# Two layers of a hybrid encoder trunk: the FFN's down-projection groups of 4, 4, 5, 5, 4 chunks in place of 5, 5, 5, 4, 3

## The chip, the core and the metric

One NeuronCore of a Trainium2 chip runs the whole kernel. The metric is the device time of one execution in microseconds (us). The kernel before takes 1569.97 us, the median of three runs between 1569.14 and 1570.35.

## What is computed

The reference runs two layers over 512 tokens of width 1024, in float32. A layer is a normalised input, three branches (two kinds of attention and a pooling branch), gates, an output projection, and then the part that the change touches, a gated MLP with 2816 hidden channels:

```python
hf = rms_norm(x, ffn_norm_g[l])
u = depthwise_conv(hf @ ffn_w_up[l], ffn_conv_w[l], ffn_conv_b[l])
u_gate, u_val = u[..., :D_FF], u[..., D_FF:]
x = x + (jax.nn.silu(u_gate) * u_val) @ ffn_w_down[l]
```

## The kernel before

**Layout.** Activations stand with channels on the 128 partitions and the 512 tokens along the row. A float32 product is made of three reduced-precision ones: each operand is split into a high part (`wh`, `HH`, `ah`) and the rest (`wl`, `HL`, `al`), and `mm3` (lines 530 to 533) issues high by high, high by low and low by high. So every weight tile that arrives by DMA (`raw`, line 403) is split before TensorE can use it. ScalarE (ACT) makes the high half. The low half comes in one of three ways: a subtraction on GpSimd or VectorE (line 458), the same subtraction on VectorE for weights that VectorE has just summed (line 492), or `by_transfer` (lines 428 to 435), where ACT writes the negated high half and GpSimd's queue issues an accumulating DMA that adds the raw weight on top (line 434).

**The FFN.** The 2816 hidden channels are 22 chunks of 128. Each chunk has a gate part and a value part, both 1024 deep. They are made in one of two ways:

- A *plain* chunk (`plain`, line 1686): two parts one after the other, each 8 weight tiles by `mm3` on 512 columns, so 24 matmuls of 512 columns for a part. Each part goes into one PSUM bank, in turn of the tags acc, ST, AV with two banks each. VectorE scales it by the normalisation factor `rbc` (line 1695), and `convolve` (line 1664) follows.
- A *pair* (`product`, line 1701): gate and value of a chunk by Winograd's seven products of a 2 by 2 block multiplication, in the order 11, 12, 1, 22, 2, 4, 3. Each product is 4 weight tiles by `mm3` on 256 columns: 12 matmuls of 256 columns. Three of the seven weight blocks are split by transfer (`fh`, `fl`, slots of their own), four are sums or differences that VectorE makes first (line 486). ACT sets partial products aside (`sx`, line 1728), VectorE adds them up (line 1736).

`convolve` is a chain that goes back and forth between ACT and VectorE: ACT scales (`a<-u`), VectorE adds the two neighbours (line 307, two instructions), ACT applies silu to a gate part; for a value part VectorE multiplies by the gate (`a<-a,a`), ACT writes the high half of the result (`act` or `ah`), VectorE the low half (`act` or `al`). Then TensorE may use the chunk.

**Groups.** The down projection needs all 22 chunks for each of its 8 output tiles, so it is done in groups: group g's chunks go into a PSUM bank (tags mi and S, in turn), 8 output tiles of as many blocks as the group has chunks; a block is three matmuls of 512 columns. VectorE then adds the bank to `XM` (line 1806). `SIZES` gives the chunks of each group. Group 0's chunks are plain, all others are pairs. The blocks of group g are dealt over the pairs of group g + 1, behind the products 22, 2, 4 and 3 of each pair; the order is written out by `_ffn` (lines 112 to 131):

```python
SIZES = (5, 5, 5, 4, 3)
PLACE = (0, 5, 0, 5, 0)
...
dealt = len(late) - (KEEP * SIZES[g - 1] if g == len(SIZES) - 1 else 0)
...
now = late[:dealt * (n + 1) // (c1 - c0) - dealt * n // (c1 - c0)]
...
late += [("d", g, m, i) for m in range(KC) for i in range(c1 - c0)]
```

Of the next to last group two output tiles' worth of blocks (`KEEP` is 2) is kept until after the last pair; then the last group's blocks follow. `PLACE` says where a group's finished chunks lie: `PLACE[g] + i` of 6 places, and past those in tiles of two other pools.

**Order and queues.** Each engine works through its own list in order. The lists are written by the program itself with a modelled clock (`Clock`, line 205), which decides the order in which chains of steps are emitted. Weights are split ahead of their use: 4 units ahead while plain units are near, 6 once a pair's unit comes within reach (line 515). SyncE (SP) issues the weights' DMAs in order; the first pairs' raw weights are fetched early, one 256 KB block after a plain part (line 155).

Of the kernel before, what the change touches and what calls it, by code (L numbers as in the profile page):

```python
# [40 lines left out]
PRE_A = 16  # L41
PRE_B = 8
LA, LAP, LAF = 3, 4, 6
SIZES = (5, 5, 5, 4, 3)
PLACE = (0, 5, 0, 5, 0)
ROOM = 6
KEEP = 2
FORMS = ("11", "12", "1", "22", "2", "4", "3")
# [58 lines left out]
def _groups():  # L107
    e = np.cumsum(SIZES)
    return [(int(b - n), int(b)) for n, b in zip(SIZES, e)]


def _ffn():
# [4 lines left out]
    for g, (c0, c1) in enumerate(_groups()):  # L117
        dealt = len(late) - (KEEP * SIZES[g - 1] if g == len(SIZES) - 1 else 0)
        for n, c in enumerate(range(c0, c1)):
# [14 lines left out]
def _layer_units():  # L134

    r = [("p", wd) for wd in _widths()]
    for tok in _ffn():
        if tok[0] == "u":
            r += [("u", T), ("p", T), ("next",)]
        elif tok[0] == "f":  # L140
            r.append(tok)
        elif (tok[2] * SIZES[tok[1]] + tok[3]) % 4 == 0:
            r.append(("u" if tok[1] < len(SIZES) - 1 else "p", T))
    return r


def _stream():
# [4 lines left out]
    for kind, *u in _layer_units() * L:  # L152
        if kind == "next":
            plain = (plain + 1) % (2 * SIZES[0])
            if plain and plain >= 2 * SIZES[0] - 8:
# [179 lines left out]
def trunk(ctx: ExitStack, tc: tile.TileContext, x, w, prm, gb, cst, out):  # L335
# [359 lines left out]
    def layer(l, sq, xsrc):  # L695
# [959 lines left out]
        def keep_act(c):  # L1655
            g = next(i for i, (c0, c1) in enumerate(groups) if c0 <= c < c1)
            i = c - groups[g][0]
            n = 2 * (PLACE[g] + i)
            if n < 2 * ROOM:
# [359 lines left out]
```

## Time and profile before

| What | Value |
|---|---|
| Median of three runs | 1569.97 us |
| The profiled execution's own time | 1569.55 us |
| Its span, first to last instruction | 1567.7 us |
| TensorE busy | 1546.2 us, 99% of the span |
| VectorE (DVE), ScalarE (ACT), GpSimd (POOL) busy | 1171.7, 1012.9, 809.8 us |
| First layer's FFN: group 0, plain | 433.4 to 491.4 us |
| Pairs of groups 1, 2, 3, 4 | 491.4 to 569.4, to 647.5, to 715.6, to 762.4 us |
| Last group's down projection | 762.4 to 784.8 us |
| Second layer's first pair | from 1270.49 us |

A row of the timeline gives the start, the duration, the engine, the line of the kernel, the operation, output and inputs, their shape, and in brackets how long the engine stood idle before and what ended that. A row of the chain gives start, duration and what ran. A matmul's duration in the timeline is modelled and overlaps the next one; the pace is the distance between starts.

### The profile page before, as it was taken

How to read it: one execution, taken by the hardware profiler on the slowest of the kernel's cores; microseconds unless marked ns; L12 is line 12 of the kernel's file. 1: busy time of each engine (PE TensorE's matmuls, PEld its weight loads, DVE VectorE, ACT ScalarE, POOL GpSimd, SP SyncE). 2: the span in 40 equal slices, each digit the busy share in tenths (PEclk: the TensorE clock that was granted, in tenths of full speed). 3: DMA queues.
4: the chain of work that ended last, by engine and by line, in shares of the span. 5: the costliest groups of instructions: out<-in, count | busy, mean ns of one | idle time of the engine just before them, and what ended most of it. 6: DMA issues, size and time to landing. Idle time of an engine off the chain costs nothing.

```text
span 1567.7 us, 24155 instructions
## 1 busy us (share of the span) xinstructions
PE 1546.2 (99%) x8265; PEld 1339.0 (85%) x8265; DVE 1171.7 (75%) x1932; ACT 1012.9 (65%) x1908; POOL 809.8 (52%) x822
## 2 busy tenths in 40 slices
PE   9999989999999999999999999899999999999999
PEld 8888878888878999999898888788887789999997
DVE  6867886875777888877756688768757778888785
ACT  5557766763457878777544577666635577777763
POOL 3984867764653222222488658768546533222222
PEclk9999999999999999999999999999999999999999
DMA  5432224313378877886434322343243688787863
GB/s 201 126 115 80 75 74 145 118 66 124 108 181 199 194 179 174 193 195 145 130 120 133 114 74 70 93 135 115 59 143 108 176 200 201 166 192 174 211 119 101
DMA packets 124684, 216.61 MB, mean 138 GB/s; under 512 B 29328, under 2 KB 51344, under 8 KB 124560
## 3 DMA queue, kind: packets, MB, share of 16 engines
q1 hardware_dynamic: 91152, 162.93, 32.9%
q0 software_dynamic: 28512, 51.92, 19.3%
q8 instruction: 65, 1.06, 0.3%
q10 hardware_dynamic: 4896, 0.21, 0.2%
q14 instruction: 59, 0.48, 0.1%
HBM read 149.41 MB, written 13.63 MB: 104 GB/s over the span
## 4 chain that ended last, share of the span: by engine, by line
PE 84%; DVE 7%; issue 3%; ACT 3%; POOL 2%; DMA 1%; SPq 0%; ACTq 0%; POOLq 0%; DVEq 0%
PE ps_acc L522 35%; PE ps_AV L522 16%; PE ps_ST L522 14%; PE ps_S L522 10%; PE ps_mi L522 10%; DVE XM L303 1%; DVE tt L303 1%; POOL wl L303 1%; DMA wl<-raw 1%; DVE mgl L303 1%; ACT mgh L296 1%; DVE sq L303 0%; DVE gt L307 0%; ACT wh L296 0%; DVE XM L307 0%
## 5 line engine op out<-in xcount | busy, mean ns | idle before, releaser
L303 POOL TENSOR_TENSOR wl<-raw,wh 128x512 fp32r<-128x512 f32 (+3 forms) x261 | 335.6, 1292 | 273.3 <-ACT wh L296 252.7
L296 ACT ACTIVATE wh<-raw 128x512 fp32r<-128x512 f32 (+2 forms) x453 | 265.4, 605 | 49.9 <-DVE raw L303 10.5
L434 POOL DMA_DIRECT2D wl<-raw x96 | 83.7, 872 | 246.8 <-ACT sx L296 160.4
L434 POOL DMA_DIRECT2D fl<-raw x102 | 89.2, 874 | 154.2 <-ACT fl L296 69.2
L522 PE MATMUL ps_acc<-HH,wl 128*128 128x512 f32 x416 | 163.2, 392 | 4.4 <-DMA wl<-raw 4.4
L522 PE MATMUL ps_acc<-HH,wh 128*128 128x512 f32 x416 | 163.4, 393 | 3.9 <-DVE vm L303 2.9
L522 PE MATMUL ps_acc<-HL,wh 128*128 128x512 f32 x416 | 162.8, 391 | 0.4 <-DVE HL L303 0.4
L307 DVE SCALAR_TENSOR_TENSOR a<-u,prm,a 128x511 f32<-128x511 f32 x176 | 133.7, 761 | 34.9 <-ACT a L296 34.1
L311 DVE TENSOR_REDUCE nm<-ps_S 128x1 fp32r<-128x512 f32 x128 | 87.7, 685 | 36.1 <-PE ps_S L522 34.7
L296 ACT ACTIVATE a<-u,prm 128x512 f32<-128x512 f32 x88 | 71.2, 811 | 63.2 <-DVE u L303 63.2
L522 PE MATMUL ps_acc<-tf,wh 128*128 128x256 f32 x544 | 100.1, 282 | 0.0
L522 PEld LDWEIGHTS ps_acc<-HH,wl 128*128 128x128 f32 x416 | 78.1, 188 | 23.1 <-DMA wl<-raw 6.2
L522 PEld LDWEIGHTS ps_acc<-HH,wh 128*128 128x128 f32 x416 | 78.3, 188 | 20.7 <-issue 4.4
L522 PEld LDWEIGHTS ps_acc<-tf,wh 128*128 128x128 f32 x544 | 88.5, 189 | 6.2
L522 PEld LDWEIGHTS ps_acc<-HL,wh 128*128 128x128 f32 x416 | 78.2, 188 | 17.1 <-DVE HL L303 1.1
L303 DVE TENSOR_TENSOR wl<-raw,wh 128x512 fp32r<-128x512 f32 (+2 forms) x97 | 71.7, 740 | 25.5 <-ACT wh L296 25.3
L522 PE MATMUL ps_AV<-HH,wh 128*128 128x256 f32 (+1 forms) x248 | 82.1, 331 | 0.0
L522 PE MATMUL ps_AV<-HH,wl 128*128 128x256 f32 (+1 forms) x248 | 82.0, 331 | 0.0
L522 PE MATMUL ps_AV<-HL,wh 128*128 128x256 f32 (+1 forms) x248 | 82.0, 331 | 0.0
L522 PE MATMUL ps_acc<-tf,wl 128*128 128x256 f32 x272 | 76.6, 282 | 0.0
L296 ACT ACTIVATE ps_ST<-ps_ST 128x512 f32<-128x512 f32 x86 | 49.8, 581 | 33.1 <-PE ps_ST L522 31.7
L296 ACT ACTIVATE fl<-fh 128x512 fp32r<-128x512 f32 x102 | 64.5, 633 | 3.2
(428 smaller groups left out, 4969.7 us busy)
## 6 DMA issues: line engine op xcount, KB each, us to landing
raw<-w SPq DMA_DIRECT2D x160, 512.0 KB, 3.7
raw<-w SPq DMA_DIRECT2D x140, 256.0 KB, 4.3
fl<-raw POOLq DMA_DIRECT2D x102, 256.0 KB, 5.4
wl<-raw POOLq DMA_DIRECT2D x96, 256.0 KB, 4.6
raw<-w SPq DMA_DIRECT2D x14, 384.0 KB, 3.0
XM<-x SPq DMA_DIRECT2D x16, 256.0 KB, 3.1
dtq<-tr SPq DMA_DIRECT2D x16, 192.0 KB, 1.9
dtk<-tr SPq DMA_DIRECT2D x16, 192.0 KB, 2.0
```

The costliest lines, as they stand in the source:

```text
L296: return self.eng.activation(out, in_, func, **k)
L303: return self.eng.tensor_tensor(out, *a)
L307: return self.eng.scalar_tensor_tensor(out, *a)
L311: return self.eng.tensor_reduce(out, in_, *a, **k)
L434: nc.gpsimd.dma_start(f(lo), r, accum_op=ALU.add)
L522: PE.matmul(o, lhsT=lhsT, rhs=rhs, start=start, stop=stop, skip_group_check=again)
```

## The change

Two tables of numbers change, and everything else follows from them:

```diff
-SIZES = (5, 5, 5, 4, 3)
-PLACE = (0, 5, 0, 5, 0)
+SIZES = (4, 4, 5, 5, 4)
+PLACE = (0, 4, 0, 5, 0)
```

The fifth chunk of each layer is now made by the seven products and no longer plain: four plain chunks and eighteen pairs, where there were five and seventeen. Blocks of the down projection behind the pairs: group 0's 32 over 4 pairs (40 over 5 before), group 1's 32 over 5 (40 over 5), group 2's 40 over 5 (40 over 4), group 3's 30 over 4 (24 over 3), and 10 kept with 32 of the last group behind the last pair (8 kept with 24 before). Seven raw blocks are fetched early, where there were eight; the eighth comes in its turn. Outside the two FFNs the order on every engine is the same as before.

On TensorE, in the first layer's first pair, the rows from the end of product 2 (bank acc) on. `mi` is the bank of the down projection's first output tile; the tiles `act_4671` to `act_4674` hold, three rows of 512 in each, the finished plain chunks' high and low halves in turn, so the fifth chunk's are the last of `act_4673` and the first of `act_4674`. Before:

```order
L522 MATMUL ps_acc_5180<-tf_4725,wl_5152 128x256
L522 MATMUL ps_mi_5272<-act_4672,wh_5130 128x512 x2
L522 MATMUL ps_mi_5272<-act_4672,wl_5131 128x512
L522 MATMUL ps_mi_5272<-act_4673,wh_5130 128x512 x2
L522 MATMUL ps_mi_5272<-act_4673,wl_5131 128x512
L522 MATMUL ps_AV_5223<-HH,wh_5181 128x256
...
L522 MATMUL ps_AV_5223<-HH,wl_5182 128x256
L522 MATMUL ps_mi_5272<-act_4673,wh_5201 128x512
L522 MATMUL ps_mi_5272<-act_4674,wh_5201 128x512
L522 MATMUL ps_mi_5272<-act_4673,wl_5202 128x512
```

And with the change, where the tiles are `act_4673` to `act_4675` and the last plain chunk is the fourth, the first two rows of `act_4675`:

```order
L522 MATMUL ps_acc_5092<-tf_4727,wl_5064 128x256
L522 MATMUL ps_mi_5184<-act_4674,wh_5042 128x512 x2
L522 MATMUL ps_mi_5184<-act_4674,wl_5043 128x512
L522 MATMUL ps_mi_5184<-act_4675,wh_5042 128x512 x2
L522 MATMUL ps_mi_5184<-act_4675,wl_5043 128x512
L522 MATMUL ps_AV_5135<-HH,wh_5093 128x256
```

The block that reads the last plain chunk has moved from behind product 4 (bank AV) to ahead of it: it is the fourth block of the pair, no longer the fifth.

On ACT, the rows from the split of a plain part's first weights on (`wl<-wh` is the negated high half for the accumulating DMA; `fh`, `fl` belong to the first pair). Before, where in the first layer eleven rows of splits and convolution stand between the split for part 7 (`wl_4945`) and the first pair's `fh`:

```order
L296 ACTIVATE wl_4945<-wh_4944 128x512
L296 ACTIVATE a_4938<-u_4937,prm_91 128x512
L296 ACTIVATE a_4938<-a_4938 128x512
L296 ACTIVATE wh_4984<-raw_4864 128x512
L296 ACTIVATE wh_4988<-raw_4916 128x512
L296 ACTIVATE wl_4989<-wh_4988 128x512
L296 ACTIVATE a_4982<-u_4981,prm_91 128x512
L296 ACTIVATE act_4672<-a_4982 128x512
L296 ACTIVATE wh_5029<-raw_4916 128x512
L296 ACTIVATE wh_5033<-raw_4962 128x512
L296 ACTIVATE wl_5034<-wh_5033 128x512
L296 ACTIVATE wh_5038<-raw_4962 128x512
```

And with the change, where part 7 is the last one:

```order
L296 ACTIVATE wl_4945<-wh_4944 128x512
L296 ACTIVATE wh_4949<-raw_4866 128x512
L296 ACTIVATE fh_4953<-raw_4487 128x512
L296 ACTIVATE fl_4954<-fh_4953 128x512
L296 ACTIVATE a_4938<-u_4937,prm_91 128x512
```

The first pair's rows follow the split for part 7 directly; the row order behind that point is the one that stood behind the split for part 9 (`wl_5034`) before.

## Prediction

> **What bounds the kernel now.** I read the page's first lines and its chain, then the stages of the first FFN, then what TensorE waited for in it.
>
> ```profile
> span 1567.7 us, 24155 instructions
> PE 1546.2 (99%) x8265; PEld 1339.0 (85%) x8265; DVE 1171.7 (75%) x1932; ACT 1012.9 (65%) x1908; POOL 809.8 (52%) x822
> PE 84%; DVE 7%; issue 3%; ACT 3%; POOL 2%; DMA 1%; SPq 0%; ACTq 0%; POOLq 0%; DVEq 0%
> 433.40:491.40 58.00, 55.86 (x243) 44.96 (x242) 41.19 (x63) 36.77 (x63) 28.91 (x25) 1.00 0.77 192
> 491.40:569.40 78.00, 78.00 (x541) 72.72 (x540) 64.53 (x108) 59.43 (x111) 21.70 (x25) 1.00 0.84 190
> 569.40:647.50 78.10, 78.10 (x541) 72.82 (x540) 63.94 (x109) 59.01 (x110) 21.64 (x25) 1.00 0.77 178
> 647.50:715.60 68.10, 68.10 (x457) 62.78 (x457) 52.79 (x92) 49.82 (x93) 19.06 (x22) 1.00 0.86 197
> PE ps_acc L522 <- DMA wl<-raw: 1.3, 2, 1.0
> PE ps_acc L522 <- ACT HH L296: 0.6, 1, 0.6
> PE ps_acc L522 <- DVE HL L303: 0.2, 1, 0.2
> ```
>
> TensorE is busy for 99% of the span and makes up 84% of the chain. The four stage rows (stretch and its length; busy time of PE, weight loads, DVE, ACT, POOL; clock, DMA share, GB/s) are the plain group and the pairs of groups 1, 2 and 3: in the pairs TensorE never stops, in the plain group it misses 2.14 us. The last three rows, of the first layer's FFN from 433 to 786 us, hold the waits that have a name, and all of them fall in the plain group. So time is won here only by giving TensorE less work, and lost wherever an operand is late; DVE, ACT and the DMAs count only through that.
>
> **Less work.** Each layer loses one plain chunk and gains one pair. Two plain parts, and then the seven products of one pair with one of the runs of two down blocks between them, read in the chain:
>
> ```profile
> 475.22 5.44 PE ps_ST L522 x24
> 480.66 5.44 PE ps_AV L522 x24
> ...
> 507.19 1.43 PE ps_acc L522 x12
> 508.61 1.44 PE ps_ST L522 x12
> 510.05 1.44 PE ps_AV L522 x12
> 511.49 1.44 PE ps_ST L522 x12
> ...
> 514.33 1.43 PE ps_acc L522 x12
> 515.75 1.40 PE ps_mi L522 x6
> 517.15 1.43 PE ps_AV L522 x12
> ...
> 519.97 1.43 PE ps_acc L522 x12
> ```
>
> A plain chunk takes 2 x 5.44 = 10.88 us, a pair 4 x 1.43 + 3 x 1.44 = 10.04 us. **The saving is 0.84 us a layer, 1.68 us in all.** It is small because half as many columns do not take half the time: 5.44/24 = 227 ns against 10.04/84 = 120 ns. The down projection keeps its 176 blocks a layer and its 40 additions to `XM`; they only stand elsewhere.
>
> The Trainium skill, "TensorE: Matmul & The Clock Gate", section "Back-to-back issue gap", gives N/2.4 + 2.5 ns between isolated warm matmuls, thus 216 and 109 ns; an estimate by that page is 48 x 216 - 84 x 109 ns = 1.2 us a layer. The rows above disagree (227 and 120 ns at a granted clock of 1.00), so 0.84 is what I use; by the page the whole sum below would end 0.7 us lower.
>
> **What gets late: the last plain chunk.** The first pair's down blocks read the plain chunks one after the other. These rows carry the timing in both layers: when the first pair starts, when the block of the last plain chunk starts, when ACT splits the weights for parts 7 and 9, and when DVE writes the last plain chunk's low half.
>
> ```profile
> 491.42 0.28 PE L522 MATMUL ps_acc<-HH,fh 128*128 128x256 f32 x1
> 502.81 0.63 PE L522 MATMUL ps_mi<-act,wh 128*128 128x512 f32 x2
> 468.26 0.63 ACT L296 ACTIVATE wl<-wh 128x512 fp32r<-128x512 f32 x1
> 478.34 0.63 ACT L296 ACTIVATE wl<-wh 128x512 fp32r<-128x512 f32 x1
> 500.74 0.69 DVE L303 TENSOR_TENSOR act<-a,act 128x512 fp32r<-128x512 f32 x1 [1.20 <-ACT act L296]
> ...
> 1270.49 0.28 PE L522 MATMUL ps_acc<-HH,fh 128*128 128x256 f32 x1
> 1247.19 0.63 ACT L296 ACTIVATE wl<-wh 128x512 fp32r<-128x512 f32 x1
> 1257.28 0.63 ACT L296 ACTIVATE wl<-wh 128x512 fp32r<-128x512 f32 x1
> 1279.68 0.69 DVE L303 TENSOR_TENSOR act<-a,act 128x512 fp32r<-128x512 f32 x1 [1.20 <-ACT act L296]
> ```
>
> *Needed sooner.* Before, the block starts 502.81 - 491.42 = 11.39 us into the pair. With the change it is the fourth block and stands ahead of product 4. Four products (5.75), two blocks (1.40), product 2 (1.43) and one block (0.70) come before it: 9.28 us. Its second matmul reads the low half, 0.23 later: 9.51 us.
>
> *Ready later.* Before, the low half is written at 500.74 + 0.69 = 501.43, or 10.01 us into the pair, and 9.88 in the second layer. That is already behind 9.51. Besides, ACT and DVE run behind TensorE in the plain group: they have begun late, since the factor `rbc` comes only at 452 us, and they catch up. From the split for part 7 to that for part 9 they need 10.08 us (10.09 in the second layer), TensorE for two parts 10.88. One chunk fewer is 0.80 us less caught up. As ACT's and DVE's rows behind that point keep their order, I shift them by 10.08 and TensorE by 10.88. In the first layer the low half is then ready at 491.35 and TensorE gets there at 491.42 - 10.88 + 9.51 = 490.05: **a wait of 1.30 us**. In the second layer 1270.28 against 1269.12: **1.16 us**. Together 2.46 us.
>
> The bounds: below, nothing, if the two engines close the gap themselves (or, with no lag, 0.50 and 0.37 from the order alone). Above, TensorE may wait for something else as well, which is counted only past this wait.
>
> **What else moves.** Three things meet just ahead of that wait. The last part's accumulating DMA is issued where part 7's was, at 469.31, but now the first pair's traffic is around it, as it was for part 9's:
>
> ```profile
> 469.31 0.90 POOL L434 DMA_DIRECT2D wl<-raw  x1 [0.23 <-PE ps_AV L522]
> 479.38 0.88 POOL L434 DMA_DIRECT2D wl<-raw  x1 [0.21 <-issue]
> DMA to landing us min/median/max: 3.6/5.7/6.8
> 494.30 0.68 DVE L303 TENSOR_TENSOR u<-ps_acc,rbc 128x512 f32<-128x512 f32 x1
> ```
>
> The part's third matmul is the first to use it, 475.22 + 2 x 0.23 = 475.68, or 6.4 us after the issue. The landing took at most 6.8 us in that stretch, so TensorE may wait 0.4 us. Product 22 now needs the ST bank of the last plain part, which VectorE empties with the instruction at 494.30: 494.98 - 10.08 = 484.90, while TensorE wants it at 491.42 - 10.88 + 4.31 = 484.85, a wait of 0.05. Both waits come before the block of the last chunk and VectorE's chain does not hang on them, so they only use up part of the 1.30 us. I count them as nothing; if that cover is gone they cost up to 0.45 us a layer. The eighth early block leaves SP's queue there and is issued behind the first down weights; its pair starts 15 us after the first, against a landing of at most 8.3 us in the rows below. The last group has 42 blocks behind the last pair instead of 32; TensorE has as many matmuls fewer elsewhere, and the last pair's chunk gets more time, not less.
>
> **Sum.** 2 x (-0.84) + 2.46 = +0.78 us. On the profiled execution's own 1569.55 us that is 1570.33; the runs' median stands 0.42 higher, so **1570.8 us**. Of this kernel about 0.2%, 3.1 us, can be told from no change, so this is no change. With the bounds (no wait at all; 0.45 us a layer more) the likeliest case alone spans 1568.3 to 1571.7.
>
> **Rivals.**
>
> *The wait is covered, the saving stays.* If ACT and DVE close their lag at the change of stage, only the 1.68 us count: 1568.3. For it: DVE is busy for only 41.19 of the plain group's 58.00 us. Against it are the longest waits of the two engines in that group, DVE's from 433 and ACT's from 452 us on:
>
> ```profile
> DVE a L307 <- ACT a L296: 9.6, 7, 2.8
> ACT act L296 <- DVE a L303: 6.0, 4, 2.3
> ```
>
> Each waits for the other, so the chain has little slack of its own. This case, too, is within no change.
>
> *VectorE becomes the bound, and the kernel slower.* Group 2 now has 6.4 blocks a pair, not 8. Its pairs take 10.04 + 6.4 x 0.70 = 14.5 us for TensorE, where they took 78.1/5 = 15.6, with the same VectorE work: 63.94/5 = 12.8 us. What VectorE can give up is what it waits for TensorE:
>
> ```profile
> DVE u L303 <- PE ps_AV L522: 6.3, 3, 2.5
> DVE u L303 <- ACT wl L296: 2.7, 2, 1.9
> ```
>
> These are its two longest waits in group 2's pairs; both end with product 4 and are 9.0 us together, 1.8 a pair. 1.1 are asked for. If they cannot be used, VectorE falls 1.1 us behind with each of five pairs. From about 3 us behind on (the aside of product 2 must be done within 1.40 + 1.43 + 0.70 us) TensorE stops; that leaves some 2.5 to 3 us a layer: 1576. Against it: the 1.8 us of waiting are there to be used, and 12.8 of 14.5 us leave room.
>
> *A low half lands late in the first pairs.* In the second pair one was issued at 502.30 and used at 508.69:
>
> ```profile
> 502.30 0.86 POOL L434 DMA_DIRECT2D fl<-raw  x1 [1.11 <-DMA raw<-w]
> 508.69 0.28 PE L522 MATMUL ps_ST<-HH,fl 128*128 128x256 f32 x1
> DMA to landing us min/median/max: 4.3/6.5/8.3
> ```
>
> 6.4 us are there, the median landing is 6.5 and the longest 8.3. The change reorders what shares the DMA engines there, so up to 1.9 us a layer could come on top, at one place: 1573 to 1574. Against it: with the wait of 1.3 us ahead of it TensorE comes later, and the landing has that more to spare.
>
> That the change does not do what it says is ruled out by the order: four plain chunks, then pairs.
>
> **How the numbers follow.** 1570.8 with chance 0.62; the saving alone (1568.3) 0.18; VectorE as the bound (1576) 0.10; late landings (1573.5) 0.10. Faster by over 0.2% (below 1566.8) needs a gain that no row shows, 0.03 of the second case. Slower by over 0.2% (above 1573.1) takes the third case and half of the fourth: 0.15. The rest, 0.82, is within 0.2%. The range leaves out the third case and the outer ends: 1568.0 to 1573.6.
>
> **What would show it.** Right: TensorE's longest idle time in the first pair stands before a `ps_mi` matmul that reads `act`, ended by DVE or ACT, 1.0 to 1.4 us in each layer, about 9.5 us into the pair; the seven products still take 10.04 us; ACT's split for the last plain part stands at 468.3 us. Wrong: no such wait (the saving alone), idle time of TensorE inside the pairs of group 2, or one before `fl`. If another stage than the two FFNs changes by more than a few tenths, the whole frame is wrong.

## The result, and the profile after

The changed kernel takes 1572.56 us (median; 1570.50 to 1574.86) beside 1568.99 us for the kernel before (1568.38 to 1571.22): 1.0021 times the time before, 95% interval 1.0012 to 1.0031. A second comparison on another occasion, e_after below, gave 1.0013 (1.0004 to 1.0021). So by the medians the change costs 3.6 and 1.6 us; the two intervals reach from 0.6 to 4.9. The forecast was 1570.8 us, a loss of 0.8, within 1568.0 to 1573.6: the time lies in that range, and the loss is two to four and a half times the forecast. The prediction gave a change of at most 0.2% a chance of 0.82; the two ratios are 0.21 and 0.13%.

The profiled execution took 1571.34 us. The first lines of its page:

```profile
span 1569.5 us, 24358 instructions
PE 1546.5 (99%) x8340; PEld 1342.4 (86%) x8340; DVE 1184.4 (75%) x1955; ACT 1018.4 (65%) x1920; POOL 806.0 (51%) x821
```

TensorE is busy as long as before (1546.5 against 1546.2 us); the span has grown by 1.8 us, so waits have grown. From the starts of TensorE's rows, the two FFNs took 3.0 us more than in the profile before, and the rest of the kernel 1.2 us less: the first FFN began at 432.59 us, 0.78 sooner, although ACT, VectorE and GpSimd have the same order up to there. Single executions differ by that much: e_early5 and e_ctrl below, grouped as before, reach the first FFN at 432.60 and 433.99. So the FFNs are compared by themselves. The stages of the first layer's FFN (stretch and its length; busy time of PE, weight loads, DVE, ACT, POOL; clock, DMA share, GB/s) are the plain group, the pairs of groups 1 to 4, and what follows the last pair:

```profile
432.59:479.70 47.11, 45.02 (x195) 35.97 (x194) 34.89 (x54) 30.76 (x53) 24.44 (x21) 1.00 0.74 189
479.70:543.63 63.93, 63.18 (x434) 58.16 (x432) 52.97 (x89) 47.95 (x89) 17.44 (x21) 1.00 0.84 188
543.63:617.73 74.10, 72.67 (x518) 68.32 (x516) 63.24 (x109) 56.94 (x106) 19.95 (x23) 1.00 0.82 185
617.73:695.73 78.00, 78.00 (x541) 72.72 (x540) 63.99 (x109) 59.02 (x110) 21.65 (x25) 1.00 0.81 186
695.73:756.81 61.08, 61.08 (x428) 57.14 (x427) 48.28 (x82) 45.54 (x85) 19.05 (x21) 1.00 0.63 132
756.81:786.70 29.89, 29.61 (x128) 23.61 (x127) 20.59 (x26) 14.63 (x25) 18.38 (x15) 1.00 0.43 150
```

Before, TensorE stood still only in the plain group. Now it misses 0.75 us in group 1's pairs, 1.43 in group 2's and 0.28 behind the last pair. The timeline names the three places. The first pair, in both layers (its start, the block of the last plain chunk, the next pair's start, and VectorE's low half of that chunk):

```profile
479.70 0.28 PE L522 MATMUL ps_acc<-HH,fh 128*128 128x256 f32 x1
489.89 0.50 PE L522 MATMUL ps_mi<-act,wh 128*128 128x512 f32 x1 [0.44 <-ACT act L296]
490.62 0.50 PE L522 MATMUL ps_mi<-act,wh 128*128 128x512 f32 x1 [0.23 <-DVE act L303]
496.83 0.28 PE L522 MATMUL ps_acc<-HH,fh 128*128 128x256 f32 x1
489.87 0.69 DVE L303 TENSOR_TENSOR act<-a,act 128x512 fp32r<-128x512 f32 x1 [1.20 <-ACT act L296]
...
1260.83 0.28 PE L522 MATMUL ps_acc<-HH,fh 128*128 128x256 f32 x1
1270.92 0.50 PE L522 MATMUL ps_mi<-act,wh 128*128 128x512 f32 x1 [0.44 <-ACT act L296]
1271.65 0.50 PE L522 MATMUL ps_mi<-act,wh 128*128 128x512 f32 x1 [0.23 <-DVE act L303]
1277.87 0.28 PE L522 MATMUL ps_acc<-HH,fh 128*128 128x256 f32 x1
1270.90 0.69 DVE L303 TENSOR_TENSOR act<-a,act 128x512 fp32r<-128x512 f32 x1 [1.20 <-ACT act L296]
```

The pair takes 17.13 and 17.04 us where 15.60 is its time without a wait: **1.53 and 1.44 us**, at the place that the prediction named (of it 0.25 and 0.15 us are lost ahead of product 22 already, where the prediction had 0.05). The brackets show less, 0.67 us a layer, because they count from modelled ends of matmuls; the distance between starts is the one to read.

The fifth and last pair of group 2 in the first layer (its start, the issue of product 12's low half on GpSimd's queue, the matmul that waits for it, and the next pair's start):

```profile
601.16 0.28 PE L522 MATMUL ps_acc<-HH,fh 128*128 128x256 f32 x1
596.47 0.87 POOL L434 DMA_DIRECT2D fl<-raw  x1 [1.39 <-ACT sx L296]
604.41 0.39 PE L522 MATMUL ps_ST<-HH,fl 128*128 128x256 f32 x1 [1.43 <-DMA fl<-raw]
617.73 0.28 PE L522 MATMUL ps_acc<-HH,fh 128*128 128x256 f32 x1
```

It takes 16.57 us, 1.67 more than the 14.90 that it takes without a wait (e_after, second layer). In the second layer the same pair shows no such row and takes 14.98. Then the part behind the last pair, where ten kept blocks come first (the kernel before: VectorE's neighbour additions for the last pair's gate; then the changed kernel: the same additions with GpSimd's and VectorE's other rows, and the matmul that waits for a bank):

```profile
760.94 1.61 DVE L307 SCALAR_TENSOR_TENSOR a<-u,prm,a 128x511 f32<-128x511 f32 x2 [0.89 <-ACT a L296]
...
753.39 4.73 POOL L303 TENSOR_TENSOR wl<-raw,wh 128x512 fp32r<-128x512 f32 x3 [0.26 <-ACT wh L296]
755.33 3.34 DVE L307 SCALAR_TENSOR_TENSOR a<-u,prm,a 128x511 f32<-128x511 f32 x2 [1.31 <-ACT a L296]
759.98 0.68 DVE L303 TENSOR_TENSOR XM<-ps_S,XM 128x512 f32<-128x512 f32 x1
760.72 0.73 PE L522 MATMUL ps_S<-act,wh 128*128 128x512 f32 x2 [0.28 <-DVE XM L303]
```

VectorE's two neighbour additions of the last pair take 3.34 us, where the kernel before needed 1.61 at that place. They make the addition of a bank to `XM` late, and TensorE waits for that bank.

The account, from the starts of TensorE's rows in two profiles of the changed kernel, against the kernel before (us; a block is 0.695, from a pair of 8 blocks: (15.60 - 10.04) / 8):

| Part of a FFN | first profile, layers 1 and 2 | e_after, layers 1 and 2 | forecast |
|---|---|---|---|
| Plain group, one chunk fewer | -10.94, -11.43 | -10.88, -11.43 | -10.88 each |
| One pair more | +10.04 | +10.04 | +10.04 each |
| First pair beyond 15.60 | +1.53, +1.44 | +1.49, +1.47 | +1.30, +1.16 |
| Fifth pair of group 2 beyond 14.90 | +1.67, +0.08 | +0.66, 0.00 | 0 |
| From the last pair on, beyond ten more blocks | +0.66, +0.56 | +0.65, +0.56 | 0 |
| The rest | -0.26, -0.39 | -0.24, -0.40 | 0 |
| Whole FFN | +2.70, +0.30 | +1.72, +0.24 | +0.46, +0.32 |

### The profile page after: what moved, and what is told of

Same layout as the page of the kernel before. It is cut to its first block, busy times and chain, and to the rows that moved or that the text cites. A ratio compares the mean times of both kernels' runs of the same rounds, so it can differ in the third digit from the quotient of the medians.

```text
span 1569.5 us, 24358 instructions
## 1 busy us (share of the span) xinstructions
PE 1546.5 (99%) x8340; PEld 1342.4 (86%) x8340; DVE 1184.4 (75%) x1955; ACT 1018.4 (65%) x1920; POOL 806.0 (51%) x821
## 4 chain that ended last, share of the span: by engine, by line
PE 79%; DVE 7%; ACT 4%; issue 4%; DMA 3%; POOL 2%; SPq 0%; ACTq 0%; POOLq 0%; DVEq 0%
PE ps_acc L522 35%; PE ps_AV L522 15%; PE ps_ST L522 12%; PE ps_S L522 9%; PE ps_mi L522 8%; DVE a L307 2%; POOL wl L303 1%; ACT wh L296 1%; DMA wl<-raw 1%; ACT a L296 1%; DMA raw<-w 1%; DVE XM L303 1%; DMA XM<-x 1%; DMA fl<-raw 1%; DVE tt L303 0%
## 5 line engine op out<-in xcount | busy, mean ns | idle before, releaser
L434 POOL DMA_DIRECT2D wl<-raw x88 | 76.7, 871 | 240.3 <-ACT sx L296 119.7
L434 POOL DMA_DIRECT2D fl<-raw x108 | 94.4, 874 | 168.1 <-ACT fl L296 68.2
L522 PE MATMUL ps_acc<-HH,wh 128*128 128x512 f32 x400 | 157.2, 393 | 3.7 <-DVE vm L303 2.9
L522 PE MATMUL ps_acc<-HH,wl 128*128 128x512 f32 x400 | 156.9, 392 | 3.7 <-DMA wl<-raw 3.7
L522 PE MATMUL ps_acc<-HL,wh 128*128 128x512 f32 x400 | 156.7, 392 | 0.4 <-DVE HL L303 0.4
L522 PE MATMUL ps_acc<-tf,wh 128*128 128x256 f32 x576 | 105.8, 282 | 0.0
L522 PEld LDWEIGHTS ps_acc<-tf,wh 128*128 128x128 f32 x576 | 93.7, 189 | 6.4
L303 DVE TENSOR_TENSOR wl<-raw,wh 128x512 fp32r<-128x512 f32 (+2 forms) x100 | 73.1, 732 | 17.1 <-ACT wh L296 16.6
L522 PE MATMUL ps_acc<-tf,wl 128*128 128x256 f32 x288 | 81.2, 282 | 0.0
L522 PE MATMUL ps_AV<-HH,wl 128*128 128x256 f32 (+1 forms) x240 | 78.1, 325 | 0.0
L522 PE MATMUL ps_AV<-HL,wh 128*128 128x256 f32 (+1 forms) x240 | 78.0, 325 | 0.0
```

The costliest lines, as they stand in the source:

```text
L303: return self.eng.tensor_tensor(out, *a)
L434: nc.gpsimd.dma_start(f(lo), r, accum_op=ALU.add)
L522: PE.matmul(o, lhsT=lhsT, rhs=rhs, start=start, stop=stop, skip_group_check=again)
```

## The experiments

Three theories came up in turn. Theory 1: the wait for the last plain chunk eats the saving, as forecast. Theory 2: in group 2's shorter pairs, low halves of weights land too late. Theory 3: behind the last pair, VectorE is held up by GpSimd. Each median stands beside the kernel before, run on the same occasion.

**e_after**: the changed kernel once more, no edit.

> The changed kernel once more, beside the kernel before on the same chip. Theory 1 (the wait for the last plain chunk): the first pair again takes about 17.1 and 17.0 us instead of 15.60, and all that is not the saving of 1.68 us lies there, so the times differ by about +1.3 us (3.0 - 1.7). Theory 2 (on top of that, low halves of split weights land late in the shorter pairs of group 2, at places that vary from one execution to the next): the difference is nearer to +3 us, this profile shows one or two waits of TensorE for a low half in group 2's pairs at other places than the first profile (the seventh product 12 of the first layer, 1.43 us), and the executions spread over 3 us or more where those of the kernel before spread over 2.

1571.49 us beside 1569.89, ratio 1.0013 (1.0004 to 1.0021). The first pairs took 17.09 and 17.07 us. In the first layer TensorE waited for two low halves; the second is the one of group 2:

```profile
482.88 0.39 PE L522 MATMUL ps_ST<-HH,fl 128*128 128x256 f32 x1 [0.76 <-DMA fl<-raw]
603.95 0.39 PE L522 MATMUL ps_ST<-HH,fl 128*128 128x256 f32 x1 [0.43 <-DMA fl<-raw]
```

The place in group 2 is the same as in the first profile, where theory 2 had expected another; the size varies. The wait at 482.88, in the first pair, cost nothing: the pair was no longer than in the first profile, since the wait for the last plain chunk behind it became that much shorter. The executions spread over 1569.43 to 1575.38, those before over 1567.84 to 1573.77 in more runs, which tells nothing.

**e_late4**: the last plain chunk's block behind product 4.

```diff
-toks += now[len(now) * k // len(SPOTS):len(now) * (k + 1) // len(SPOTS)]
+toks += now[len(now) * k // len(SPOTS):len(now) * (k + 1) // len(SPOTS)] if (g, n) != (1, 0) else now[(0, 1, 3, 5, 8)[k]:(0, 1, 3, 5, 8)[k + 1]]
```

> The first pair of group 1 deals its eight blocks as 1, 2, 2, 3 over the four places instead of 2, 2, 2, 2, so that the block of the last plain chunk stands behind product 4. TensorE then comes to its low half 10.94 us into the pair; from the profile of the changed kernel (9.51 us and a wait of 1.53 and 1.44) it is ready 11.04 and 10.95 us in. Theory 1: the wait goes, the first pair takes 15.6 to 15.7 us in both layers, and the time falls by 2.8 to 2.9 us against the changed kernel. Theory 2 agrees on the first pair, but leaves the waits in group 2, so the kernel still is not below the one before by the full 1.7 us. Rival (the wait only moves: what follows the block is late as well): a wait of about the same size shows before another matmul in the first two pairs, and the time stays within 0.8 us of the changed kernel.

1569.99 us beside 1569.89, ratio 0.9999 (0.9990 to 1.0008): 1.5 us less than e_after, where 2.8 was expected, with about 1 us of uncertainty on either side. The wait for `act` is gone in both layers. But the first pairs took 16.81 and 16.16 us, and the second layer's second pair 16.06, which is 2.2 us too long where e_after's were 3.0. What TensorE waits for now are low halves:

```profile
482.77 0.39 PE L522 MATMUL ps_ST<-HH,fl 128*128 128x256 f32 x1 [0.67 <-DMA fl<-raw]
1277.34 0.38 PE L522 MATMUL ps_ST<-HH,fl 128*128 128x256 f32 x1 [0.20 <-DMA fl<-raw]
```

The view of the tile `fl` tells how long the three low halves issued between 469 and 477 us took to land, counted from the issue of the DMA:

```profile
DMA to landing us min/median/max: 8.1/9.8/10.4
```

In the changed kernel's first profile the first pair left them 9.6, 9.3 and 8.8 us from issue to use. In e_after the delay was there too, hidden by the wait behind it. With 0.54 and 0.84 us lost in the fifth pairs of group 2, this execution's two FFNs take 706.15 us together, those of e_after 706.16; the fall of the median does not show in this profile. So by the profile the rival came closer than theory 1: most of the wait only moved, to an earlier product. By the median the result lies between the two.

**e_early5**: the kernel before, with the fifth chunk's block moved ahead of product 2.

```diff
-toks += now[len(now) * k // len(SPOTS):len(now) * (k + 1) // len(SPOTS)]
+toks += now[len(now) * k // len(SPOTS):len(now) * (k + 1) // len(SPOTS)] if (g, n) != (1, 0) else now[(0, 5, 6, 7, 8)[k]:(0, 5, 6, 7, 8)[k + 1]]
```

> The kernel before, with five plain chunks, but with the first pair's eight blocks dealt as 5, 1, 1, 1, so that the fifth plain chunk's block stands ahead of product 2. TensorE comes to its low half 5.75 + 4 x 0.70 + 0.23 = 8.78 us into the pair; it is ready 10.01 and 9.88 us in. Theory 1: the wait alone, without the saving and without shorter pairs: 1.23 and 1.10 us, so +2.3 us over the kernel before; if the reckoning is short by as much as it was in the changed kernel (0.23 and 0.28), +2.8. Theory 2 has nothing to add here, since group 2's pairs keep their length: no wait for a low half in group 2. Rival (the order of the blocks costs nothing, since the chain closes up): within 0.5 us of the kernel before.

1569.71 us beside 1569.89, ratio 1.0000 (0.9991 to 1.0009). By the time this is the rival's result; in the trace the wait came at the place expected, but at half the size: the first pairs took 16.17 and 16.19 us instead of 15.60.

```profile
490.61 0.28 PE L522 MATMUL ps_acc<-HH,fh 128*128 128x256 f32 x1
491.48 0.69 DVE L303 TENSOR_TENSOR u<-ps_acc,rbc 128x512 f32<-128x512 f32 x1
499.09 0.69 DVE L303 TENSOR_TENSOR act<-a,act 128x512 fp32r<-128x512 f32 x1 [1.39 <-ACT act L296]
499.83 0.50 PE L522 MATMUL ps_mi<-act,wh 128*128 128x512 f32 x1 [0.23 <-DVE act L303]
```

The expectation failed because it kept VectorE's order. VectorE empties the last plain part's bank 0.87 us into the pair here; before it did so 2.88 us in (at 494.30, the row in the prediction). By the code, the program emits what a block needs ahead of the block, so an earlier block can pull the chain forward; that cause was read, not tried apart. The low half was ready 9.17 us into the pair, not 10.01. In the changed kernel the order did not change: there VectorE empties that bank 3.73 us into the pair. The 1.2 us of waits are too little for the medians to show.

**e_laf7** and **e_laf7in**: the weights of pairs split 7 units ahead, everywhere, or only until the last pair comes near.

```diff
-LA, LAP, LAF = 3, 4, 6
+LA, LAP, LAF = 3, 4, 7
```

```diff
-n = LAF if any(k not in "pu" for k in kinds_) else LAP if "u" in kinds_[:2] else LA
+n = LAF + any(u[0] not in "pu" for u in units[j + 14:j + 24]) if any(k not in "pu" for k in kinds_) else LAP if "u" in kinds_[:2] else LA
```

> The changed kernel with the weights of pairs split 7 units ahead of their use instead of 6, so that each low half is issued a product (1.43 us) or so sooner. Theory 2: low halves in group 2's pairs then have 1.4 us to spare, no wait before one is left in group 2, and the time falls by 1 to 2 us against the changed kernel, with executions closer together. Theory 1 alone: nothing to gain there, the time stays within 0.5 us or rises. Rival: the split that ACT does sooner stands ahead of the last plain chunk's chain, so the first pair's wait grows by one split (0.63 to 1.3 us a layer), and the time rises by 1 to 2.5 us.

> As e_laf7, but back to 6 units ahead before the last pair of each layer, where the profile of e_laf7 lost 1.8 us a layer. Theory 2 (late low halves cost the changed kernel something on top of the wait for the last plain chunk): the pairs as in e_laf7, first pairs 16.8 us instead of 17.1, no wait for a low half in group 2's pairs, and the part behind the last pair as in the changed kernel, 45.4 to 45.5 us; that is 1.0 to 1.3 us below the second profile of the changed kernel, some 1570.4. Theory 1 alone: within 0.4 us of the changed kernel. Rival: the loss behind the last pair comes from somewhere else than the splits of the last pair and stays, so the time stays near e_laf7's 1573.5.

e_laf7: 1573.48 us beside 1569.89, ratio 1.0028 (1.0017 to 1.0038). Theory 2's waits are gone, the fifth pair of group 2 takes 14.88 and 14.90 us and the first pairs 16.8, but the time rises, and not where the rival put it. From the last pair's start on it takes 47.3 us instead of 45.5:

```profile
750.66 0.38 PE L522 MATMUL ps_AV<-HH,wh 128*128 128x256 f32 x1 [0.49 <-ACT sx L296]
761.38 0.73 PE L522 MATMUL ps_S<-act,wh 128*128 128x512 f32 x2 [1.07 <-DVE XM L303]
```

e_laf7in takes that part back to 45.5 us: 1571.16 beside 1569.73, ratio 1.0007 (0.9998 to 1.0016). No wait for a low half is left in group 2 (14.88 and 14.90 us again), which is theory 2's step. But in the first layer's first pair TensorE waited 0.87 us for one, and that pair took 17.59. The two FFNs make 706.06 us against e_after's 706.16: what was gained in one place was lost in another, and the medians cannot tell the kernels apart.

**e_44455** and **e_45544**: other groupings with the same four plain chunks.

```diff
-SIZES = (4, 4, 5, 5, 4)
+SIZES = (4, 4, 4, 5, 5)
```

```diff
-SIZES = (4, 4, 5, 5, 4)
-PLACE = (0, 4, 0, 5, 0)
+SIZES = (4, 5, 5, 4, 4)
+PLACE = (0, 5, 0, 5, 0)
```

> Four plain chunks and eighteen pairs like the changed kernel, in groups of 4, 4, 4, 5, 5: group 2's pairs have 8 blocks each again, and the shorter pairs, of 6 and 7 blocks, are group 3's (32 blocks over 5) and group 4's (30 over 5). The first pair is dealt as in the changed kernel, so its wait stays, 17.0 to 17.1 us in both layers. Theory 2 (a shorter pair leaves the low halves no room): no wait for one in group 2, and one or two of 0.3 to 1.6 us in the pairs of group 3 or 4. Rival (it is the place, some 120 us into the FFN, whatever the length of the pairs): a wait for a low half again in the pair that starts near 600 us, none in groups 3 and 4. Time 1571 to 1573 either way.

> Groups of 4, 5, 5, 4, 4: the same four plain chunks, but their 32 blocks are dealt over five pairs, so the first pair has 6, dealt 1, 2, 1, 2, and the last plain chunk's block stands behind product 4, 10.94 us into the pair for its low half; it is ready 10.9 us in. Theory 1: no wait of more than 0.2 us for the last plain chunk. Theory 2: the short pairs are now the first ones, where the low halves are the latest, so TensorE waits for low halves there, 0.7 to 1.6 us a layer. Together 1569.5 to 1571, below the changed kernel by 1 to 2 us. Rival (the first pair's loss is not the block's place but the missing fifth plain chunk, whose time ACT and VectorE lack): first pairs longer than 14.2 us by 1.2 us or more through a wait for another product of ACT or VectorE.

e_44455: 1573.18 us beside 1569.73, ratio 1.0020 (1.0011 to 1.0029). The first pairs took 17.06 and 16.91 us. From the last pair on it lost 1.3 us a layer beyond its blocks (50.3 against 14.21 + 50 x 0.695 = 49.0), which no expectation had; 0.70 of it stands at one matmul that waits for an aside of ACT. No low half was waited for in groups 2 to 4, so by its waits the run decides for neither theory 2 nor its rival. The time from issue to use favours theory 2. In group 3's fifth pair, the last of its short ones, product 12's low half has as little of it as in group 2's fifth pair of the changed kernel. The rows of e_44455, and then those of group 2's fifth pair in the kernel before:

```profile
660.55 0.87 POOL L434 DMA_DIRECT2D fl<-raw  x1 [1.36 <-ACT sx L296]
666.89 0.38 PE L522 MATMUL ps_ST<-HH,fl 128*128 128x256 f32 x1
...
623.77 0.88 POOL L434 DMA_DIRECT2D fl<-raw  x1 [0.60 <-ACT sx L296]
633.60 0.28 PE L522 MATMUL ps_ST<-HH,fl 128*128 128x256 f32 x1
```

That is 6.3 us from issue to use, against 9.8 in the kernel before; in the changed kernel's group 2 the same product had 6.4 us in the second layer (1377.53 to 1383.89), and in e_45544, whose short pairs are group 1's, the fifth of them has 6.4 (533.13 to 539.49). So the shortage goes with a run of short pairs, wherever that stands. Whether TensorE then waits depends on the landing, which differs between executions: the three low halves of that fifth pair took 4.3, 7.2 and 7.9 us in the first profile.

e_45544: 1576.61 us beside 1569.73, ratio 1.0045 (1.0032 to 1.0057), over 5 us above the expectation. TensorE does not wait for the last plain chunk any more, as theory 1 said. Low halves were late, in the second layer's second pair by 0.29 us and in its fifth by 1.13. The first pairs lost 0.76 and 0.61 us beyond 14.22, of which the rows name 0.26 and 0.16. The large loss was in none of the theories: from the last pair's start on, 2.9 us a layer more than its blocks need (44.9 against 14.21 + 40 x 0.695 = 42.0):

```profile
1322.40 0.39 PE L522 MATMUL ps_ST<-HH,fl 128*128 128x256 f32 x1 [1.13 <-DMA fl<-raw]
760.72 0.73 PE L522 MATMUL ps_S<-act,wh 128*128 128x512 f32 x2 [1.55 <-DVE XM L303]
```

**e_best**: e_late4 and e_laf7in together.

> e_late4 and e_laf7in together: the first pair's blocks dealt 1, 2, 2, 3, and splits 7 units ahead up to the last pair. Theories 1 and 2 together: first pairs of 15.6 to 15.8 us in both layers, no wait for a low half in the pairs, so that the saving of 1.68 us is left: 1568.0 to 1568.8, 0.05 to 0.12% below the kernel before, and 3 us below the changed kernel. Rival (with both waits gone TensorE meets a third one: VectorE's sum for product 22 or ACT's asides, 0.3 us in e_laf7, grow): 1569.5 to 1570.5.

1569.54 us beside 1569.73, ratio 0.9999 (0.9990 to 1.0007): the rival's time, though not by its cause. The second layer's first pair came down to 15.96 us, but in the first layer a low half landed late again (0.70 us) and the pair took 16.78. And 0.6 us a layer remained from the last pair on, which led to theory 3.

**e_kept**: the changed kernel with three of the last group's weight tiles split by transfer.

```diff
-r.append(("u" if tok[1] < len(SIZES) - 1 else "p", T))
+r.append(("u" if tok[1] < len(SIZES) - 1 or tok[2] < 3 else "p", T))
```

> The changed kernel with the first three weight tiles of each layer's last group split by transfer instead of by GpSimd's subtraction. In the changed kernel three such subtractions (4.73 us of GpSimd from 753.39 on) stand beside VectorE's two neighbour additions in the last pair, which take 3.34 us instead of 1.54; VectorE's addition of a bank to XM then starts at 759.98, and TensorE waits for that bank (0.28 us shown at 760.72, 0.43 by the distance of starts, and 0.1 for starting again). Theory 3 (VectorE is held by GpSimd's subtractions): the two additions take 1.5 to 1.6 us, the addition to XM comes 1.5 to 1.8 us sooner against TensorE, the wait for the bank goes, and the part from the last pair's start to the end of the FFN takes 44.8 to 45.0 us instead of 45.5 in both layers: 1.1 us less in all. Rival (VectorE is slow there for another reason, its own queue): 3.3 us and the wait stay. Second rival: the transfers land late, and TensorE waits for a low half in the last group instead.

1569.78 us beside 1569.33, ratio 1.0007 (0.9998 to 1.0016), 0.0006 or 1 us below e_after's ratio, which the intervals cannot tell apart but the rows can. From the last pair's start on 44.98 and 44.89 us instead of 45.52 and 45.43, and no wait for the bank:

```profile
752.51 0.87 POOL L434 DMA_DIRECT2D wl<-raw  x1 [1.24 <-ACT wl L296]
754.12 1.54 DVE L307 SCALAR_TENSOR_TENSOR a<-u,prm,a 128x511 f32<-128x511 f32 x2 [1.98 <-ACT a L296]
756.97 0.68 DVE L303 TENSOR_TENSOR XM<-ps_S,XM 128x512 f32<-128x512 f32 x1
```

With GpSimd's subtractions gone the two additions take 1.54 us. Theory 3 is shown, at 0.54 us a layer. (In the same profile the second layer's fifth pair of group 2 waited again for a low half, 15.72 us.) The Trainium skill, "SBUF — State Buffer", section "SBUF: two separate sides", says that a VectorE instruction with two inputs in SBUF and a GpSimd instruction that reads SBUF exclude each other, each for its whole length. The trace agrees: 3.34 us beside the three subtractions, 1.54 without.

**e_best2** and **e_best2b**: all remedies, twice, with 7 units ahead from the first pairs' approach on.

```diff
-LA, LAP, LAF = 3, 4, 6
+LA, LAP, LAF = 3, 4, 7
-n = LAF if any(k not in "pu" for k in kinds_) else LAP if "u" in kinds_[:2] else LA
+n = LAF - all(u[0] in "pu" for u in units[j + 14:j + 24]) if any(k not in "pu" for k in kinds_) else LAP if "u" in kinds_[:2] else LA
```

(and the edits of e_late4 and e_kept)

> All remedies together: the first pair's blocks dealt 1, 2, 2, 3; splits 7 units ahead from the first pairs' approach on and 6 from before the last pair; the last group's first three weight tiles split by transfer. By the accounts of e_late4, e_laf7 and e_kept: first pairs of 15.6 to 15.9 us in both layers, no wait for a low half, 44.9 us from the last pair's start on. Then the saving of 1.68 us is left with about 0.7 us of small waits of the kernel before that are gone as well: 1567.0 to 1568.0, 0.1 to 0.17% below the kernel before. Rival (each remedy is paid for elsewhere, as e_best's first pair was): 1568.5 to 1569.5, the same as the kernel before.

> e_best2 once more, on the same chip as the control: 0.05 to 0.15% below the kernel before again, FFNs of 350.5 to 351.2 and 351.4 to 352.0 us, no wait of TensorE for a low half in the pairs. Rival (the first result was a lucky draw): level with the kernel before.

1568.32 us beside 1569.33, ratio 0.9990 (0.9981 to 0.9999), and 1567.99 beside 1570.01, ratio 0.9989 (0.9980 to 0.9998): faster than the kernel before by a little, between the expectation and its rival the first time, and by its median as expected the second. In the first layer's FFN of e_best2, between 479.5 and 785 us, TensorE waited by name for one thing:

```profile
PE ps_ST L522 <- DVE u L303: 0.3, 1, 0.3
```

The first pairs took 15.9 to 16.2 us, and no low half was late in either layer's pairs. The two FFNs make 702.60 and, in the second run, 702.96 us, against 704.20 in the kernel before: 1.60 and 1.24 less. That this is near the saving of 1.68 is in part chance: in e_best2 the first pairs still lose 1.0 us, and the second layer's plain group was 0.6 us shorter than one chunk less accounts for.

Over all profiles of this grouping theory 2 holds: with splits 7 units ahead product 12's low half has 7.4 us instead of 6.4, and all ten fifth pairs of group 2 take at most 14.90 us; with 6, five of eight take 15.4 to 16.6.

**e_ctrl**: the kernel before with the splits and the last group as in e_best2.

> The control: the kernel before, in groups of 5, 5, 5, 4, 3, with the two of e_best2's remedies that apply to it (splits 7 units ahead up to the last pair, the last group's first three weight tiles by transfer). If e_best2's time is the saving of one plain chunk a layer, freed of the new waits, the remedies give nothing here, since no such wait stands in the kernel before: within 0.5 us of it, 1.0 us or more above e_best2. Rival (the remedies speed up any grouping): 1 us or more below the kernel before, and level with e_best2.

1571.70 us beside 1570.01, ratio 1.0011 (1.0002 to 1.0020). Neither the expectation, within 0.5 us of the kernel before, nor the rival came: the remedies do not speed up the old grouping; they slow it. A wait for the bank comes up that was not there. Ahead of it the one subtraction that is left to GpSimd there stands beside VectorE's scaling by `rbc`, which takes 2.26 us:

```profile
764.31 1.65 POOL L303 TENSOR_TENSOR wl<-raw,wh 128x512 fp32r<-128x512 f32 x1
764.25 2.26 DVE L303 TENSOR_TENSOR u<-u,rbc 128x512 f32<-128x512 f32 x1
767.17 0.73 PE L522 MATMUL ps_S<-act,wh 128*128 128x512 f32 x2 [0.88 <-DVE XM L303]
1547.06 0.73 PE L522 MATMUL ps_S<-act,wh 128*128 128x512 f32 x2 [0.85 <-DVE XM L303]
```

In the changed kernel that scaling took 0.69 us (at 759.37), in the kernel before 1.01 (at 763.24). So the new loss looks like theory 3's again, at another instruction; no run took that subtraction away. The control's pairs took what they took before, to 0.02 us. So what e_best2 has over the kernel before does not come from the remedies as such, though a control that loses elsewhere proves less than one that stays level.

## Why the prediction was right, and where it was not

**What bounds the kernel, and the saving: right.** Pairs without a wait still take 15.60 us with eight blocks; the plain group became 10.88 to 10.94 us shorter in the first layer. That is the prediction's 0.84, and not the 1.2 us that came out by the Trainium skill's rule ("TensorE: Matmul & The Clock Gate", section "Back-to-back issue gap"). In the second layer the plain group became 0.55 us shorter still; its named waits, for weights above all, were 2.7 us instead of 3.2. That need not come from the change: e_ctrl, with five plain chunks, has 0.52 of it too.

**The wait for the last plain chunk: right in place and cause, 0.5 us too small.** ACT's split for the last part stood at 467.47; the whole FFN had begun 0.78 us sooner, and from its start it is the forecast to 0.01 us. The low half was ready 10.86 and 10.76 us into the pair (forecast 10.81 and 10.67). The rest, about 0.2 us a layer, lies between VectorE's end and TensorE's full pace: 490.56 to 490.62, and 0.57 us from that matmul to the next product where two matmuls take 0.46. A wait costs somewhat more than the lateness of its operand. The prediction left that out.

**"Counted as nothing", ahead of the wait: right while the wait stood.** e_after had a low half 0.76 us late there and the pair was no longer for it. Product 22's wait came as well, 0.25 and 0.15 us in the first profile. With the wait gone, e_late4 showed the price of the missing cover: 1.21 and 0.56 us, more than the 0.45 named, because landings took up to 10.4 us where the prediction went by the 8.3 of its row.

**The last group, counted as nothing: wrong.** The prediction counted blocks and the time that the last pair's chunk has. It did not look at which engine splits the last group's weights, and when. The groups' sizes had moved three GpSimd subtractions beside VectorE's additions. That cost 0.6 us a layer.

**VectorE as the bound in group 2: wrong as priced, but the lag behind it was real.** TensorE kept the pace of 14.2 and 14.9 us a pair; no sum of VectorE stopped it, and 1576 did not come. But ACT's waits for VectorE in these pairs changed. Its largest waits there, before and after:

```profile
ACT a L296 <- DVE a L307: 8.1, 5, 2.2
ACT a L296 <- DVE u L303: 6.5, 5, 1.3
ACT wh L296 <- DVE raw L303: 1.5, 3, 0.9
```

```profile
ACT a L296 <- DVE u L303: 6.2, 6, 1.7
ACT a L296 <- DVE a L307: 5.5, 5, 2.0
ACT wh L296 <- DVE raw L303: 4.0, 4, 2.3
```

ACT waits for VectorE's sums of weights 4.0 us instead of 1.5. It makes the negated high halves in its own order, and GpSimd's queue can add to them only then; so product 12's low half is issued 6.4 us ahead of its use at the end of group 2, not 9.8. That VectorE's lag is what makes it late is read from these rows; no run tried it. The rival looked for the stop at VectorE's results. It came at a transfer queued behind them, and cost 0 to 1.7 us, differently in each execution. A late low half was among the rivals, but in the first pairs: the prediction looked where the kernel before had the least time to spare, 6.4 us in its second pair, and in that pair of the changed kernel nothing was late.

**Its own signs.** Of the signs that it named as right, the wait before `ps_mi`, the 10.04 us of the seven products and ACT's split came, the wait above its 1.0 to 1.4 us; in e_after's first layer the longest idle time stood before `fl` instead. Of the signs of being wrong, idle time inside group 2's pairs, before `fl`, came as well. So two of its cases, to which it gave separate chances, came together: the likeliest one and late landings, these in another group. The last sign, another stage changed by more than a few tenths, was too strict for one execution against another: the first FFN began 0.78 us sooner with the same order ahead of it.

**The sum.** +0.8 us was forecast; the two profiled FFNs make +3.0 and +2.0, the medians +3.6 and +1.6. Of the difference between 3.0 and 0.8, 1.75 is group 2's fifth pair, 1.2 the end, 0.5 the wait itself, and 1.2 goes the other way (shorter waits in the plain group, and pairs of the kernel before that were slightly slower than counted). So the range held partly by luck: two terms put at nothing cost 3.0 us in the first profile and 1.9 in e_after, and 1.2 that nobody had counted came back. Without it the median of 1572.56 would stand near 1573.8, just outside the range.

**Open.** Why the low halves of the first pair take 8 to 10 us to land, and differently each time, was not tried; in e_best2, where the first of them is issued some 3 us sooner, it lands after 4.2 us in both layers. Nor was the end of e_45544 taken apart: its rows name 1.9 us of the 2.9, the longest 1.55.

## What to carry to other kernels

When the bounding engine's stage becomes shorter, list for every operand the time from its issue to its use, before and after, not only the busy time of the other engines: here 9.8 us became 6.4 while VectorE still had idle time. A wait that covers others is worth less than its size when it is taken away, so look for what stands ahead of it first. And where a regrouping moves work, look at what each engine then does side by side at the borders of stages, not only at how much it does.

## What the runs showed of the hardware

- VectorE's `a<-u,prm,a` (two instructions) took 3.34 us beside three GpSimd subtractions and 1.54 without them; the subtractions took 1.58 us each on average there, and 1.29 to 1.30 alone.
- An accumulating DMA of 256 KB for the first layer's first pair landed after 7.8 to 10.4 us in three runs (the changed kernel, e_after, e_late4), and after 6.7 to 8.2 in the kernel before; those for group 2's fifth pair landed after 4.3 to 7.9 in the changed kernel's first profile.
- After a wait TensorE needed about 0.1 us more than the distance of its matmuls to be back at its pace (0.57 us for two matmuls that take 0.46, in the changed kernel's first pair).
